# Two weight sums of a Strassen product in buffers of their own

## The chip, the cores and the metric

The kernel runs on one core of a Trainium2 chip. The metric is the device time of one execution in microseconds (us). Before the change it was 2573.67 us, the median of 3 runs (2573.44 to 2575.31).

The engines of the core work on their own, each through a list of instructions in a fixed order, and wait for each other by semaphores: PE multiplies matrices into PSUM, DVE and POOL work elementwise, ACT casts and applies functions, SP issues the transfers from and to HBM.

## What is computed

One layer of a streaming encoder on 512 frames of 2048 channels, all in float32: a combined input projection, stick-breaking attention, a spatial gating unit, two output projections and a squared-ReLU MLP. The change lies in the MLP, which is the last of it:

```python
D_MODEL = 2048
SEQ = 512
D_FF = 4 * D_MODEL

        x = x + merged @ w_out[l]

        h2 = rms_norm(x, g_ff[l])
        x = x + jnp.square(jax.nn.relu(h2 @ w_ff1[l])) @ w_ff2[l]
```

## The kernel before

**Two parts for each operand.** PE multiplies in a shorter float type. So each operand is split into a rounded part, hi, and the rest, lo: ACT casts the block to hi and DVE subtracts hi from the block (`split_to`, lines 103 and 104; for weights of the other products `weight`, lines 90 and 92). A product is three matmuls, hi by hi, hi by lo and lo by hi (`mm3`, lines 68 to 70). Which of lines 69 and 70 reads the weights' lo depends on the side on which the weights stand: in `strassen` it is line 69 (weights on the right), in the first MLP product line 70.

**The MLP's loop** (lines 631 to 649) runs over 16 chunks of 512 hidden channels. In each chunk, twice (g = 0 and 1, here the even and the odd product): `hidden` computes 256 channels of the next chunk (four weight loads, 96 matmuls; a relu on DVE, line 603, and a square on ACT, line 604), and then `strassen` multiplies the current chunk by a block of w_ff2 of 512 rows and 1024 columns and adds it into x. The last chunk has no `hidden`.

**The Strassen product** (lines 140 to 188) is Winograd's form: seven products of quarters instead of eight. The four quarters w11, w12, w21, w22 of the weights are loaded with SP in this order (line 156). The seven products stand in a fixed order, y11, y21, m7, m6, y22, m4, m5, with 12 matmuls each. y11, m4 and y21 take w11, w22 and w12 as they are loaded. The other four take sums of quarters that POOL makes by `plus` (line 165):

- m7 takes w11 + w21, written in the place of w11
- m6 takes that sum + w22, in a buffer of its own, sc
- y22 takes sc + w12, written in the place of w12
- m5 takes w21 + w22, written in the place of w21

Each is recorded right ahead of the product that takes it. A sum in the place of w11 has to wait until w11 has been split for y11.

Products y11, m6 and m5 accumulate in one pair of PSUM banks, m7 and m4 in another; y21 and y22 use a third, one after the other. After each product, `evac_y` adds the banks into x (line 643, on DVE), for m5 twice; the next product on the same banks adds to them once DVE has read them. The pieces w_hi and w_lo go round in 6 buffers, so three blocks are in flight.

**The other factors** (`factors`, lines 610 to 625) are made once a chunk: POOL makes four sums of the activations for each of two pairs (lines 615 to 618), and ACT and DVE split 7 factors of each pair (ys, 128x256). These fall into the odd product of the chunk before, since the activations are ready only there.

**What sets the order.** The program is written in the order above, and a scheduler then fixes the order of each engine's list with a timing model of its own. Buffers come from pools. A pool hands its buffers out again in the order in which they come free, and who takes one waits for the last reader of what was in it. The pool `slots` has 72 buffers of 128x512, of which x takes 16, the normed input of the MLP 32, and the rest goes round among activations, sums and factors. The pool `spare` (10 such buffers, for the first transposed inputs and the last merged blocks) is given up ahead of the MLP, and the pool `whole` (line 590: 5 buffers of 128x1024, for the four quarters and sc) takes its place.

## Time and profile before

| | |
|---|---|
| median of 3 runs | 2573.67 us |
| the profiled execution, its own time | 2574.17 us |
| its span, first to last instruction | 2572.5 us |
| granted clock of PE | 1.0 |
| instructions | 28610 |
| share of 16 DMA engines' time on loads | 32.7% |

The page has six parts: busy time by engine; the span in 40 slices; DMA queues; the chain of work that ended last; the costliest groups of instructions; and DMA issues. A group's row names the line, engine, operation, output<-inputs with their shape, and how many; behind the first bar its busy time in us and the mean of one in ns; behind the second the engine's idle time just before these instructions and what ended it. A row of the timeline gives start and length in us, engine, line, operation, tiles, how many such instructions follow each other, and in brackets the idle time before it. A matmul's length in the rows is longer than the step from one to the next, since matmuls are pipelined.

### The profile page before, as it was taken

The page shows a single profiled execution, that of the slowest core. Times are in us where ns is not written, and L with a number is a line of the kernel's source. Part 1 is how long each engine was busy: PE and PEld are TensorE (multiplying, and loading weights), DVE is VectorE, ACT ScalarE, POOL GpSimd, SP SyncE. Part 2 cuts the span into 40 slices and gives each one's busy share as a digit, 9 for nine tenths or more (in the row PEclk, how much of TensorE's full clock was granted, in tenths as well). Part 3 has the DMA queues.
Part 4 walks back from the last instruction along what each step waited for, and adds up shares of the span by engine and source line. Part 5 has one row for each costly group of instructions (what it writes and reads, how often), then busy time and mean ns, then how long its engine had stood idle before and what let it go on. Part 6 is the DMA issues. An engine that isn't in the chain of part 4 may idle for free.

```text
span 2572.5 us, 28610 instructions
## 1 busy us (share of the span) xinstructions
PE 2532.1 (98%) x11306; PEld 2082.1 (81%) x11306; DVE 1438.7 (56%) x1806; ACT 852.9 (33%) x1172; POOL 589.0 (23%) x379
## 2 busy tenths in 40 slices
PE   8999999999999999999999999999999999999998
PEld 7888888888888888888878777887778777877786
DVE  4555563333335333333475767667666767576759
ACT  5333342222223222223333333333332334233333
POOL 0211110000211000100223242414342333324244
PEclk9999999999999999999999999999999999999999
DMA  5332323333332333434233323233323333332323
GB/s 172 90 91 74 90 64 99 93 97 98 115 115 78 99 101 93 129 107 133 88 110 95 115 87 111 89 115 97 101 90 107 102 95 99 98 115 82 114 68 121
DMA packets 169574, 259.83 MB, mean 101 GB/s; under 512 B 8368, under 2 KB 77024, under 8 KB 169440
## 3 DMA queue, kind: packets, MB, share of 16 engines
q1 hardware_dynamic: 169440, 258.01, 32.7%
q8 instruction: 89, 1.46, 0.2%
q14 instruction: 45, 0.37, 0.0%
HBM read 253.78 MB, written 4.19 MB: 100 GB/s over the span
## 4 chain that ended last, share of the span: by engine, by line
PE 87%; DVE 10%; issue 1%; ACT 1%; DMA 0%; POOL 0%; SPq 0%; DVEq 0%; ACTq 0%; POOLq 0%
PE f L69 9%; PE f L68 9%; PE f L70 9%; PE q L69 6%; PE q L70 6%; PE q L68 6%; DVE w_lo L104 4%; DVE ys L104 3%; DVE x L643 3%; PE xo L70 2%; PE xo L69 2%; PE xo L68 2%; PE gb L68 2%; PE gb L70 2%; PE gb L69 2%; PE ga L68 2%
## 5 line engine op out<-in xcount | busy, mean ns | idle before, releaser
L92 DVE TENSOR_TENSOR w_lo<-w_raw,w_hi 128x1024 fp32r<-128x1024 f32 x336 | 414.2, 1233 | 686.5 <-ACT w_hi L90 677.7
L90 ACT CAST w_hi<-w_raw 128x1024 fp32r<-128x1024 f32 x336 | 353.7, 1053 | 988.8 <-PE q L69 190.0
L104 DVE TENSOR_TENSOR w_lo<-w_raw,w_hi 128x1024 fp32r<-128x1024 f32 x192 | 281.9, 1469 | 255.8 <-ACT w_hi L103 255.8
L68 PE MATMUL f<-h2T_hi,w_hi 128*128 128x512 f32 x1024 | 398.6, 389 | 0.0
L69 PE MATMUL f<-h2T_lo,w_hi 128*128 128x512 f32 x1024 | 398.5, 389 | 0.0
L70 PE MATMUL f<-h2T_hi,w_lo 128*128 128x512 f32 x1024 | 397.9, 391 | 0.0
L69 PE MATMUL q<-w_lo,ys 128*128 128x512 f32 x896 | 352.8, 394 | 26.4 <-DVE w_lo L104 26.3
L165 POOL TENSOR_TENSOR w_raw<-w_raw 128x1024 f32<-128x1024 f32 x64 | 183.1, 2862 | 820.0 <-DVE w_lo L104 820.0
L70 PE MATMUL q<-w_hi,ys 128*128 128x512 f32 x896 | 349.0, 389 | 0.0
L643 DVE TENSOR_TENSOR x<-x,q 128x512 f32<-128x512 f32 x512 | 331.0, 676 | 2.3 <-PE q L70 0.6
L103 ACT CAST w_hi<-w_raw 128x1024 fp32r<-128x1024 f32 x192 | 201.8, 1053 | 391.2 <-PE f L69 290.3
L68 PE MATMUL q<-w_hi,ys 128*128 128x512 f32 x896 | 324.0, 391 | 1.5 <-DVE x L643 1.2
L69 PEld LDWEIGHTS q<-w_lo,ys 128*128 128x128 f32 x896 | 168.1, 188 | 74.1 <-DVE w_lo L104 40.0
L70 PEld LDWEIGHTS f<-h2T_hi,w_lo 128*128 128x128 f32 x1024 | 192.2, 188 | 44.2 <-DVE w_lo L92 4.6
L69 PEld LDWEIGHTS f<-h2T_lo,w_hi 128*128 128x128 f32 x1024 | 192.2, 188 | 40.1
L68 PEld LDWEIGHTS f<-h2T_hi,w_hi 128*128 128x128 f32 x1024 | 192.3, 188 | 39.4
L68 PEld LDWEIGHTS q<-w_hi,ys 128*128 128x128 f32 x896 | 168.1, 188 | 40.3 <-issue 3.5
L70 PEld LDWEIGHTS q<-w_hi,ys 128*128 128x128 f32 x896 | 168.3, 188 | 33.8
L68 PE MATMUL gb<-hT_hi,w_hi 128*128 128x512 f32 x256 | 100.3, 392 | 0.2 <-DVE gb L413 0.2
L68 PE MATMUL xo<-w_hi,mT_hi 128*128 128x512 f32 x256 | 100.5, 393 | 0.0
L68 PE MATMUL ga<-hT_hi,w_hi 128*128 128x512 f32 x256 | 100.4, 392 | 0.0
L69 PE MATMUL ga<-hT_lo,w_hi 128*128 128x512 f32 x256 | 100.0, 391 | 0.0
(199 smaller groups left out, 3919.4 us busy)
## 6 DMA issues: line engine op xcount, KB each, us to landing
w_raw<-in_w_ff_dram SPq DMA_DIRECT2D x256, 512.0 KB, 3.7
w_raw<-in_w_in_dram SPq DMA_DIRECT2D x144, 512.0 KB, 3.7
w_raw<-in_w_out_dram SPq DMA_DIRECT2D x32, 512.0 KB, 3.7
w_raw<-in_w_oa_dram SPq DMA_DIRECT2D x16, 512.0 KB, 3.7
w_raw<-in_w_ob_dram SPq DMA_DIRECT2D x16, 512.0 KB, 3.6
x<-in_x_dram SPq DMA_DIRECT2D x16, 256.0 KB, 5.3
out_dram<-x SPq DMA_DIRECT2D x16, 256.0 KB, 2.2
xq<-in_x_dram SPq DMA_DIRECT2D x12, 256.0 KB, 6.4
```

What stands on the lines that cost most here:

```text
L68: nc.tensor.matmul(o, lhsT=lh[0], rhs=rh[0], start=start, stop=False, **kw)
L69: nc.tensor.matmul(o, lhsT=lh[0], rhs=rh[1], start=False, stop=False, **kw)
L70: nc.tensor.matmul(o, lhsT=lh[1], rhs=rh[0], start=False, stop=stop, **kw)
L90: nc.scalar.copy(out=hi, in_=raw)
L92: nc.vector.tensor_tensor(out=lo, in0=raw, in1=f32(hi), op=ALU.subtract)
L103: nc.scalar.copy(out=hi, in_=src)
L104: nc.vector.tensor_tensor(out=lo, in0=src, in1=f32(hi), op=ALU.subtract)
L165: nc.gpsimd.tensor_tensor(out=o, in0=a, in1=b, op=ALU.add)
L643: nc.vector.tensor_tensor(out=a, in0=a, in1=o, op=op)
```

## The change

Two of the four sums get buffers of their own. w11 + w21 goes to a new buffer, sa, so w11 stays whole, and the sum for m6 is made from sa. All sums but that for y22 are recorded ahead of the first product, and so depend on loads alone and on a free buffer; the sum for y22, which still goes in the place of w12, is recorded behind w12's split for y21. The order of the products, the operands of each product and the number of sums stay as they were. The pool `whole` has 6 buffers instead of 5. For that, `spare` has 12 and `slots` 70; the transposed inputs in `spare` are 6 pairs instead of 5.

```diff
-SLOTS = 72
-SPARE = 10
+SLOTS = 70
+SPARE = 12
...
-        sc = whole("w_sum")
+        sa, sc = whole("w_sum"), whole("w_sum")
...
-        made = {"m7": lambda: plus(w11, w11, w21), "m6": lambda: plus(sc, w11, w22),
-                "y22": lambda: plus(w12, sc, w12), "m5": lambda: plus(w21, w21, w22)}
-        take = {"y11": w11, "y21": w12, "m7": w11, "m6": sc, "y22": w12, "m4": w22, "m5": w21}
+        plus(sa, w11, w21)
+        plus(sc, sa, w22)
+        plus(w21, w21, w22)
+        take = {"y11": w11, "y21": w12, "m7": sa, "m6": sc, "y22": w12, "m4": w22, "m5": w21}
...
-            if name in made:
-                made[name]()
             hi, lo = piece("w_hi"), piece("w_lo")
             split_to(hi, lo, take[name])
+            if name == "y21":
+                plus(w12, sc, w12)
...
-    state["whole"] = ctx.enter_context(tc.tile_pool(name="whole", bufs=5))
+    state["whole"] = ctx.enter_context(tc.tile_pool(name="whole", bufs=6))
```

Lines behind the constants and ahead of the loop of products keep their numbers; from there on, a line has a number higher by one (643 becomes 644).

How this moves instructions is shown at three places. All are in one chunk, around its odd product, the one that starts at 1912.55 us in the profile of before; numbers behind a name tell buffers apart.

POOL, from the last sum of the factors to the next product's weight sums; in brackets the semaphores waited for (DMAHW those of loads). Before:

```order
L617 TENSOR_TENSOR m_13789<-relu_13609,m_13788 128x256 [waits Pool_49]
L165 TENSOR_TENSOR w_raw_13943<-w_raw_13943,w_raw_13947 128x1024 [waits DMAHW7_49,DMAHW1_49,DVE_49]
L165 TENSOR_TENSOR w_sum_13951<-w_raw_13943,w_raw_13949 128x1024 [waits DMAHW2_49,Pool_49]
L165 TENSOR_TENSOR w_raw_13947<-w_raw_13947,w_raw_13949 128x1024
L165 TENSOR_TENSOR w_raw_13945<-w_sum_13951,w_raw_13945 128x1024 [waits DMAHW0_49,DVE_49,Pool_49]
```

Now:

```order
L618 TENSOR_TENSOR m_13805<-relu_13624,m_13804 128x256 [waits Pool_49]
L165 TENSOR_TENSOR w_sum_13967<-w_raw_13959,w_raw_13963 128x1024 [waits DMAHW7_49,DMAHW1_49,DVE_49]
L165 TENSOR_TENSOR w_raw_13963<-w_raw_13963,w_raw_13965 128x1024 [waits DMAHW2_49,Pool_49]
L165 TENSOR_TENSOR w_sum_13968<-w_sum_13967,w_raw_13965 128x1024 [waits DVE_49]
L165 TENSOR_TENSOR w_raw_13961<-w_sum_13968,w_raw_13961 128x1024 [waits DMAHW0_49,DVE_49,Pool_49]
```

The sum for m5 has moved ahead of that for m6. The first sum's wait for DVE was one for the split of w11 of its own product; now it is one for the split of w22 (for m4) of the product before, whose buffer it takes. The third sum waits likewise for the split for m5 of the product before. The last, for y22, waits for w12's split of its own product, as before.

DVE in the odd product, from the split for m4 to that for m5 (w_lo from w_raw; ys are the next factors, x2 the additions into x). Before:

```order
L104 TENSOR_TENSOR w_lo_13723<-w_raw_13618,w_hi_13722 128x1024
L104 TENSOR_TENSOR ys_13803<-m_13788,ys_13803 128x256
L104 TENSOR_TENSOR ys_13806<-relu_13609,ys_13806 128x256
L104 TENSOR_TENSOR ys_13809<-m_13789,ys_13809 128x256
L643 TENSOR_TENSOR x2_8284<-x2_8284,q_13626 128x512
L104 TENSOR_TENSOR w_lo_13742<-w_raw_13616,w_hi_13741 128x1024
```

Now:

```order
L104 TENSOR_TENSOR w_lo_13740<-w_raw_13633,w_hi_13739 128x1024
L104 TENSOR_TENSOR ys_13810<-relu_13621,ys_13810 128x256
L104 TENSOR_TENSOR ys_13813<-relu_13624,ys_13813 128x256
L104 TENSOR_TENSOR ys_13816<-m_13804,ys_13816 128x256
L644 TENSOR_TENSOR x2_8282<-x2_8282,q_13644 128x512
L104 TENSOR_TENSOR ys_13819<-m_13804,ys_13819 128x256
L644 TENSOR_TENSOR x2_8284<-x2_8284,q_13645 128x512
L104 TENSOR_TENSOR w_lo_13758<-w_raw_13631,w_hi_13757 128x1024
```

Three factors and the addition of m6's first tile, which stood ahead of m4's split, now stand behind it. From the split for m7 to that for m4 DVE's list was: the split for m7, 2 additions, the split for m6, a factor, an addition, 4 factors, an addition, 2 factors, the split for y22, an addition, a factor, an addition, 2 factors, an addition, the split for m4. It is now: the split for m7, 2 additions, 3 factors, an addition, the split for m6, 3 factors, an addition, the split for y22, a factor, 2 additions, the split for m4.

DVE from the split for m5 to the first split of the hidden product that follows (line 92). Before:

```order
L104 TENSOR_TENSOR w_lo_13742<-w_raw_13616,w_hi_13741 128x1024
L104 TENSOR_TENSOR ys_13812<-m_13789,ys_13812 128x256
L643 TENSOR_TENSOR x2_7986<-x2_7986,q_13706 128x512
L643 TENSOR_TENSOR x2_7988<-x2_7988,q_13707 128x512
L92 TENSOR_TENSOR w_lo_13821<-w_raw_13817,w_hi_13819 128x1024
```

Now:

```order
L104 TENSOR_TENSOR w_lo_13758<-w_raw_13631,w_hi_13757 128x1024
L644 TENSOR_TENSOR x2_7986<-x2_7986,q_13723 128x512
L104 TENSOR_TENSOR ys_13822<-relu_13624,ys_13822 128x256
L104 TENSOR_TENSOR ys_13825<-m_13805,ys_13825 128x256
L104 TENSOR_TENSOR ys_13828<-m_13805,ys_13828 128x256
L644 TENSOR_TENSOR x2_7988<-x2_7988,q_13724 128x512
L92 TENSOR_TENSOR w_lo_13837<-w_raw_13833,w_hi_13835 128x1024
```

Three factors are left for this stretch where one was. On PE, y22's and m4's matmuls keep their pattern (both banks by hi, then lo). At the end of the odd product PE's list is now: m5's first matmul on one bank, two matmuls of the hidden product, m5's first on the other bank, then m5's other ten. SP's list of loads is the same; w11 now takes the buffer of the w11 before, w12 that of sa, w21 that of sc, and w22 that of w12.

## The prediction

> **What bounds the kernel now.** I read the page's first and fourth part, then the groups, then the timeline of one stretch of the second MLP product.

> ```profile
> PE 2532.1 (98%) x11306; PEld 2082.1 (81%) x11306; DVE 1438.7 (56%) x1806; ACT 852.9 (33%) x1172; POOL 589.0 (23%) x379
> ...
> PE 87%; DVE 10%; issue 1%; ACT 1%; DMA 0%; POOL 0%; SPq 0%; DVEq 0%; ACTq 0%; POOLq 0%
> ...
> L69 PE MATMUL q<-w_lo,ys 128*128 128x512 f32 x896 | 352.8, 394 | 26.4 <-DVE w_lo L104 26.3
> ...
> L165 POOL TENSOR_TENSOR w_raw<-w_raw 128x1024 f32<-128x1024 f32 x64 | 183.1, 2862 | 820.0 <-DVE w_lo L104 820.0
> ```

> PE is busy 98% of the span, so little can be won: the span less PE's busy time is 40.4 us. Of that, 26.3 us are waits for the splits of the blocks of the second product (w_lo, line 104). POOL's 820.0 us of waiting for a split, which the change addresses by name, is idle time of an engine that is busy 23%, and costs nothing by itself.

> The end follows from how long a chunk of the last loop takes. The timeline of PE shows where three chunks in a row start their second product of the odd kind (g = 1):

> ```profile
> 1828.52 0.39 PE L68 MATMUL q<-w_hi,ys 128*128 128x512 f32 x1
> ...
> 1912.55 0.39 PE L68 MATMUL q<-w_hi,ys 128*128 128x512 f32 x1
> ...
> 1994.77 0.39 PE L69 MATMUL f<-h2T_lo,w_hi 128*128 128x512 f32 x1
> ...
> 1996.58 0.39 PE L68 MATMUL q<-w_hi,ys 128*128 128x512 f32 x1
> 1996.81 0.39 PE L69 MATMUL q<-w_lo,ys 128*128 128x512 f32 x1
> ```

> A chunk lasts 84.03 us, both times. From 1994.77 to 1996.81 there are nine steps from matmul to matmul, so one takes 0.2267 us. A chunk has 360 (two hidden products of 96, two Strassen products of 84), 81.6 us. So 2.4 us are lost in each chunk, and they are lost in the product that starts at 1912.55, which I call S:

> ```profile
> 1923.43 0.61 PE L68 MATMUL q<-w_hi,ys 128*128 128x512 f32 x2
> 1924.99 0.50 PE L69 MATMUL q<-w_lo,ys 128*128 128x512 f32 x1 [0.94 <-DVE w_lo L104]
> ...
> 1927.41 0.94 PE L68 MATMUL q<-w_hi,ys 128*128 128x512 f32 x3
> 1928.92 0.50 PE L69 MATMUL q<-w_lo,ys 128*128 128x512 f32 x1 [0.58 <-DVE w_lo L104]
> ```

> At y22 the third matmul could start at 1923.43 + 0.45 and starts 1.11 us later; at m4 the fourth could start at 1927.41 + 0.68 and starts 0.83 later. That is 1.94 of the 2.4. Both wait for DVE, and DVE waits there for nothing: it works through a queue of splits (w_lo), splits of the next factors (ys) and additions into x, and its neighbour POOL slows it.

> **How DVE and POOL get in each other's way.** First POOL's rows of this stretch, then DVE's:

> ```profile
> 1906.51 2.40 POOL L165 TENSOR_TENSOR w_sum<-w_raw 128x1024 f32<-128x1024 f32 x1
> 1908.86 3.39 POOL L165 TENSOR_TENSOR w_raw<-w_raw 128x1024 f32<-128x1024 f32 x1
> 1912.21 2.40 POOL L165 TENSOR_TENSOR w_raw<-w_sum,w_raw 128x1024 f32<-128x1024 f32 x1
> ...
> 1918.75 0.81 POOL L617 TENSOR_TENSOR m<-relu,m 128x256 f32<-128x256 f32 x1
> ```

> ```profile
> 1908.17 1.82 DVE L104 TENSOR_TENSOR w_lo<-w_raw,w_hi 128x1024 fp32r<-128x1024 f32 x1 [4.21 <-ACT w_hi L103]
> ...
> 1913.66 2.03 DVE L104 TENSOR_TENSOR w_lo<-w_raw,w_hi 128x1024 fp32r<-128x1024 f32 x1 [0.22 <-ACT w_hi L103]
> 1915.62 1.27 DVE L643 TENSOR_TENSOR x<-x,q 128x512 f32<-128x512 f32 x2
> 1916.81 1.26 DVE L104 TENSOR_TENSOR w_lo<-w_sum,w_hi 128x1024 fp32r<-128x1024 f32 x1
> ...
> 1918.88 0.67 DVE L643 TENSOR_TENSOR x<-x,q 128x512 f32<-128x512 f32 x1
> ...
> 1919.81 1.84 DVE L104 TENSOR_TENSOR ys<-m,ys 128x256 fp32r<-128x256 f32 x2
> 1921.57 0.96 DVE L104 TENSOR_TENSOR ys<-relu,ys 128x256 fp32r<-128x256 f32 x1
> ...
> 1923.05 0.75 DVE L104 TENSOR_TENSOR ys<-m,ys 128x256 fp32r<-128x256 f32 x2
> 1923.72 1.21 DVE L104 TENSOR_TENSOR w_lo<-w_raw,w_hi 128x1024 fp32r<-128x1024 f32 x1
> 1924.86 0.68 DVE L643 TENSOR_TENSOR x<-x,q 128x512 f32<-128x512 f32 x1
> ```

> Alone, a split takes 1.21 us (1923.72). The one at 1908.17 takes 1.82: it gets through only when the sum that POOL began at 1906.51 ends at 1908.91. The next sum begins at 1908.86 and takes 3.39 instead of 2.40: it moves only when that split ends, at 1909.99. So the two take turns, a whole instruction each. After 1909.99 the sum needs until 1912.25: it bars DVE for **2.2 us**. A small factor sum of POOL bars it for 0.55: two splits of factors take 1921.57 - 1919.81 = 1.76 us beside POOL's factor sums and 1923.72 - 1923.05 = 0.67 without them, 0.88 against 0.335 each. An addition into x reads PSUM and isn't barred: 0.67 at 1918.88, inside the POOL instruction of 1918.75. In a row of its own, DVE steps on by 1.14 for a split (1923.72 to 1924.86) and by 0.60 for an addition (1915.62 to 1916.81, two).

> [...]

> **The change, part by part.** It removes and adds no instruction on PE, DVE, ACT or POOL and no load; it moves them.

> *The sums.* Before, the four sums for a product wait for the split of its first block, and the first three run during the hidden product, where DVE has slack (idle 4.21 us before the split of 1908.17). Now three of them need only loads and a free buffer. The buffers go round in the order of release: the first sum takes that of w22, free when m4 of the product before is split; the second needs the load of w22; the third takes that of w21, free when m5 is split. The load of w21 is issued behind the split for m6 and lands long before that:

> ```profile
> w_raw<-in_w_ff_dram SPq DMA_DIRECT2D x256, 512.0 KB, 3.7
> ```

> So three sums leave the quiet hidden product and run **in the middle of the product before it**, from m4's split on, one after another, on DVE's busiest stretch.

> *Before m4.* By the new order I add up DVE's queue in the odd product. The split for m7 starts, as now, behind ACT's cast, at S + 1.11; it ends at 2.25, since no sum bars it. The second addition waits for the product y11, whose last matmul starts at S + 2.5 and ends 0.39 later: 2.9 to 3.5. From there to the end of m4's split stand 7 splits of factors (2.35), 4 additions (2.4), 3 block splits (3.4), and POOL's factor sums, of which I let two bar for their whole 0.55 and one for 0.1 (1.2; in the nearest rows, from 1919.81 to 1922.45, three of three do): S + 12.85. Products start every 12 x 0.2267 = 2.72 us. y22's split is through at 9.65 and needed at 10.88 + 0.45; m4's is through at 12.85 and needed at 14.05. **Both old stalls go.** The bounds of the barring are 0 and 7 x 0.55: m4's split comes 1.2 earlier or 2.65 later; all that follows moves with it.

> *After m4.* One split of a factor passes (13.2). Then the first sum bars until 15.4, a factor passes (15.75), the second sum bars until 17.95, a factor passes (18.3). The addition of m6's first tile ends at 18.9, a factor at 19.2, the second addition at 19.8, the split for m5 at 20.95. PE is due for m5 at S + 16.3. Its first matmul adds into the bank that the first addition reads: it waits until 18.9, 2.6 us. Two matmuls of the hidden product stand next, then m5's on the other bank (0.25 lost), then the first that needs the split: 0.95 lost. In all 3.8, and m5 ends at 23.25.

> *The hidden product.* Its third matmul needs a split on DVE. From 20.95: an addition (21.55), the third sum bars until 23.25, three factors (24.25), an addition (24.85), the split (26.0). PE comes there at 23.25: 2.8 lost. The next split is needed 5 us later, and there DVE is in time.

> So a chunk loses 6.6 us in place of 2.4: **+4.2**. In the even product there are no factors to split; one sum delays m5's split by about 1 us, and it has 2 us to spare, since three pieces are in flight: I take nothing.

> *The other two edits.* The main pool has 70 slots, not 72, so new factors wait for older ones to be used up; ACT casts them ahead of the blocks. The cast for m6 then ends by S + 3.75 for a use at 8.6: hidden, by nearly 5 us. At the program's start the order of transposes and squares moves a little. PE idles there for the first loads, which stay:

> ```profile
> L276 PE MATMUL xT<-ident,xk 128*128 128x128 f32 x16 | 4.1, 424 | 4.3 <-DMA xk<-in_x_dram 4.3
> L226 PE MATMUL gp<-ident,gm 16*128 16x16 f32 x1 | 0.3, 256 | 2.7 <-DMA gm<-in_g_mix_dram 2.7
> ```

> I take nothing for it, and at most 2 us either way.

> *The end.* The last odd product but one starts at 1912.55 + 7 x 84.03 = 2500.8. From the first, at 1324.3, there are 14 chunks: 14 x 4.2 = 58.8. Behind 2500.8 there is no hidden product, and ACT waits for sums:

> ```profile
> L69 PE MATMUL q<-w_lo,ys 128*128 128x512 f32 x84 | 33.6, 400 | 5.1 <-DVE w_lo L104 5.0
> ...
> L68 PE MATMUL q<-w_hi,ys 128*128 128x512 f32 x84 | 30.2, 392 | 1.5 <-DVE x L643 1.2 <-ACT w_hi L103 0.2
> ...
> L103 ACT CAST w_hi<-w_raw 128x1024 fp32r<-128x1024 f32 x16 | 16.5, 1050 | 28.0 <-POOL w_raw L165 13.9 <-PE q L69 11.4 <-DVE x L643 1.5
> ```

> PE loses 6.6 us there (these groups are from 2500 us on). Sums that are ready earlier take some of it away: I take -3, between -6.6 and +5.

> Sum: 58.8 - 3 = +56. The profiled run took 2574.17 us (span 2572.5), the median of the three runs 2573.67: **2629**.

> **The rivals.** [...] 0.07. (2) *The change doesn't do what it says:* w21's load comes so late that the sums still run in the hidden product. It would have to land 6 us after its issue behind m6's split (S + 6.4), not 3.7. Then 2545 to 2575. 0.04. (3) *Partly:* the barring falls on other instructions and costs about what is won, 2570 to 2600; 0.05. (4) *Slower still:* the two missing slots hold back a cast on ACT, and with it m4's split; each us costs 14: 2645 to 2660. The cast would have to lose its 5 us first. 0.06.

> **How the numbers follow.** The forecast has 0.78. The hold is between 2.0 and 2.4 (8 us either way), the queue before m4 between -1.2 and +2.65 per chunk (-17, +37), the end between -4 and +8; not all at one end. So 2600 to 2652, which leaves out rivals 1 to 3 and a little of the forecast, 0.18 in all. About 0.2% can be told from no change here. Slower: 0.78 + 0.06 + 0.02 of rival 3 = 0.86; within 0.2%: 0.03 of rival 3 and 0.02 of rival 2, 0.05; faster: 0.07 + 0.02 = 0.09.

> **What would show it.** A chunk of 88.2 us instead of 84.03; no wait of PE at y22 and m4, but one at m5 for an addition (line 644) and one of the hidden product's matmul on line 70 for line 92; POOL's sums of 2.4 us or more beginning 13 us after the odd product's start, with splits of factors of over 2 us beside them; and POOL's wait for w_lo shorter than 820. Splits of 0.4 us beside such sums would make the prediction wrong, and so would sums that still start in the hidden product.

## The result, and the profile after

The changed kernel takes **2640.37 us** (median of four runs, 2634.77 to 2642.11); the kernel before took 2573.93 beside it (2573.44 to 2575.31). The ratio is 1.0253, with a 95% interval of 1.0236 to 1.0271: slower. The profiled run is the shortest of the four, 2634.77, with a span of 2632.7; 60.2 us more than the span before.

First the page of the changed kernel: the engines' busy time, the chain that ended last, and three groups of PE's matmuls (busy us, mean ns, then PE's idle time ahead of them and who ended it).

```profile
PE 2555.9 (97%) x11306; PEld 2097.1 (80%) x11306; DVE 1506.7 (57%) x1806; ACT 856.8 (33%) x1172; POOL 600.5 (23%) x379
...
PE 82%; DVE 13%; issue 3%; ACT 1%; DMA 0%; POOL 0%; SPq 0%; DVEq 0%; ACTq 0%; POOLq 0%
...
L70 PE MATMUL f<-h2T_hi,w_lo 128*128 128x512 f32 x1024 | 401.0, 394 | 23.2 <-DVE w_lo L92 23.2
...
L69 PE MATMUL q<-w_lo,ys 128*128 128x512 f32 x896 | 357.7, 399 | 11.2 <-DVE w_lo L104 11.1
...
L68 PE MATMUL q<-w_hi,ys 128*128 128x512 f32 x896 | 329.9, 398 | 30.0 <-DVE x L644 29.5
```

The 26.3 us of waiting for splits of blocks (line 104) went down to 11.1. Two new waits came: 29.5 for the addition into x (line 644) and 23.2 for the hidden product's split (line 92). Besides, PE's busy time rose by 23.8 us for the same 11306 matmuls. Most of it comes from "half-clock" matmuls: 83 that step on by 0.427 us instead of 0.2267, 16.6 us in all (the granted clock is 0.50 there, as for the 9 matmuls from 1700.66 to 1704.08); the last section is about them. POOL's waits, from the view that groups waits (us in all, how often, the longest):

```profile
POOL w_raw L165 <- issue: 578.1, 31, 23.2
POOL w_sum L165 <- DVE w_lo L104: 219.4, 31, 11.2
```

The 820.0 us that POOL's sums waited for splits are 219.4 now. POOL isn't idle for less time, though: 578.1 us more stand ahead of the sum for y22, which still waits for w12's split and which the view puts under "issue". What changed is the place: three of the four sums now run in another stretch, and the kernel lost by it. One odd product shows how. PE first, from the product's start S = 1944.55 to the start of the next chunk's odd product:

```profile
1944.55 0.39 PE L68 MATMUL q<-w_hi,ys 128*128 128x512 f32 x1
...
1963.17 0.48 PE L68 MATMUL q<-w_hi,ys 128*128 128x512 f32 x1 [2.14 <-DVE x L644]
...
1965.15 0.80 PE L69 MATMUL q<-w_lo,ys 128*128 128x512 f32 x1 [0.21 <-DVE w_lo L104]
...
1970.30 0.50 PE L70 MATMUL f<-h2T_hi,w_lo 128*128 128x512 f32 x1 [1.80 <-DVE w_lo L92]
...
2032.58 0.39 PE L68 MATMUL q<-w_hi,ys 128*128 128x512 f32 x1
```

A chunk of 88.03 us. No wait at y22 and m4 is left; PE waits at m5, for an addition and then for the split, and in the hidden product's third matmul. POOL in the same stretch, and DVE:

```profile
1946.09 1.60 POOL L618 TENSOR_TENSOR m<-relu,m 128x256 f32<-128x256 f32 x1
...
1952.59 2.11 POOL L619 TENSOR_TENSOR m<-relu 128x256 f32<-128x256 f32 x1
...
1955.48 1.61 POOL L618 TENSOR_TENSOR m<-relu,m 128x256 f32<-128x256 f32 x1
1957.05 2.58 POOL L165 TENSOR_TENSOR w_sum<-w_raw 128x1024 f32<-128x1024 f32 x1
1959.71 2.43 POOL L165 TENSOR_TENSOR w_raw<-w_raw 128x1024 f32<-128x1024 f32 x1
1965.17 2.38 POOL L165 TENSOR_TENSOR w_sum<-w_sum,w_raw 128x1024 f32<-128x1024 f32 x1 [3.03 <-DVE w_lo L104]
```

```profile
1952.56 1.21 DVE L104 TENSOR_TENSOR w_lo<-w_raw,w_hi 128x1024 fp32r<-128x1024 f32 x1
1953.69 0.41 DVE L104 TENSOR_TENSOR ys<-m,ys 128x256 fp32r<-128x256 f32 x1
...
1955.22 1.26 DVE L104 TENSOR_TENSOR w_lo<-w_raw,w_hi 128x1024 fp32r<-128x1024 f32 x1
1956.41 3.50 DVE L104 TENSOR_TENSOR ys<-relu,ys 128x256 fp32r<-128x256 f32 x2
1959.84 2.59 DVE L104 TENSOR_TENSOR ys<-m,ys 128x256 fp32r<-128x256 f32 x1
1962.35 0.68 DVE L644 TENSOR_TENSOR x<-x,q 128x512 f32<-128x512 f32 x1
...
1963.88 1.21 DVE L104 TENSOR_TENSOR w_lo<-w_raw,w_hi 128x1024 fp32r<-128x1024 f32 x1
...
1965.62 2.22 DVE L104 TENSOR_TENSOR ys<-relu,ys 128x256 fp32r<-128x256 f32 x1
...
1969.03 1.21 DVE L92 TENSOR_TENSOR w_lo<-w_raw,w_hi 128x1024 fp32r<-128x1024 f32 x1
```

The first sum begins 12.5 us after S, and each of the three sums has one split of a factor beside it that gets through only as it ends: 3.50 for a pair, 2.59 and 2.22 for one. DVE's queue behind them is late.

### The profile page after: what moved, and what is told of

It reads as the page before. It is cut to its first block, busy times and chain, and to the rows that moved or that the text cites. A ratio compares the mean times of both kernels' runs of the same rounds, so it can differ in the third digit from the quotient of the medians.

```text
span 2632.7 us, 28646 instructions
## 1 busy us (share of the span) xinstructions
PE 2555.9 (97%) x11306; PEld 2097.1 (80%) x11306; DVE 1506.7 (57%) x1806; ACT 856.8 (33%) x1172; POOL 600.5 (23%) x379
## 4 chain that ended last, share of the span: by engine, by line
PE 82%; DVE 13%; issue 3%; ACT 1%; DMA 0%; POOL 0%; SPq 0%; DVEq 0%; ACTq 0%; POOLq 0%
PE f L70 9%; PE f L69 9%; PE f L68 9%; DVE ys L104 5%; PE q L68 5%; PE q L69 5%; PE q L70 5%; DVE x L644 4%; DVE w_lo L104 3%; PE xo L70 2%; PE xo L69 2%; PE xo L68 2%; PE gb L68 2%; PE gb L70 2%; PE gb L69 2%
## 5 line engine op out<-in xcount | busy, mean ns | idle before, releaser
L92 DVE TENSOR_TENSOR w_lo<-w_raw,w_hi 128x1024 fp32r<-128x1024 f32 x336 | 446.3, 1328 | 653.9 <-ACT w_hi L90 642.2
L90 ACT CAST w_hi<-w_raw 128x1024 fp32r<-128x1024 f32 x336 | 353.6, 1052 | 1056.2 <-PE q L69 225.4
L70 PE MATMUL f<-h2T_hi,w_lo 128*128 128x512 f32 x1024 | 401.0, 394 | 23.2 <-DVE w_lo L92 23.2
L68 PE MATMUL f<-h2T_hi,w_hi 128*128 128x512 f32 x1024 | 402.1, 393 | 0.0
L69 PE MATMUL f<-h2T_lo,w_hi 128*128 128x512 f32 x1024 | 401.9, 393 | 0.0
L69 PE MATMUL q<-w_lo,ys 128*128 128x512 f32 x896 | 357.7, 399 | 11.2 <-DVE w_lo L104 11.1
L104 DVE TENSOR_TENSOR w_lo<-w_raw,w_hi 128x1024 fp32r<-128x1024 f32 x160 | 216.3, 1352 | 252.4 <-ACT w_hi L103 252.4
L68 PE MATMUL q<-w_hi,ys 128*128 128x512 f32 x896 | 329.9, 398 | 30.0 <-DVE x L644 29.5
L70 PE MATMUL q<-w_hi,ys 128*128 128x512 f32 x896 | 354.3, 395 | 0.0
L103 ACT CAST w_hi<-w_raw 128x1024 fp32r<-128x1024 f32 x160 | 168.8, 1055 | 371.0 <-PE f L69 254.6
L70 PEld LDWEIGHTS f<-h2T_hi,w_lo 128*128 128x128 f32 x1024 | 194.0, 189 | 70.4 <-DVE w_lo L92 30.2
L68 PEld LDWEIGHTS q<-w_hi,ys 128*128 128x128 f32 x896 | 170.7, 190 | 74.9 <-issue 33.5
L69 PEld LDWEIGHTS f<-h2T_lo,w_hi 128*128 128x128 f32 x1024 | 194.2, 190 | 40.9
L68 PEld LDWEIGHTS f<-h2T_hi,w_hi 128*128 128x128 f32 x1024 | 194.2, 190 | 39.5
L69 PEld LDWEIGHTS q<-w_lo,ys 128*128 128x128 f32 x896 | 171.8, 192 | 56.1 <-DVE w_lo L104 20.7
L165 POOL TENSOR_TENSOR w_raw<-w_sum,w_raw 128x1024 f32<-128x1024 f32 x32 | 76.8, 2401 | 591.2 <-issue 578.1
L70 PEld LDWEIGHTS q<-w_hi,ys 128*128 128x128 f32 x896 | 171.9, 192 | 35.3
L165 POOL TENSOR_TENSOR w_sum<-w_raw 128x1024 f32<-128x1024 f32 x32 | 79.7, 2491 | 189.1 <-DVE w_lo L104 176.8
L165 POOL TENSOR_TENSOR w_sum<-w_sum,w_raw 128x1024 f32<-128x1024 f32 x32 | 91.5, 2858 | 44.0 <-DVE w_lo L104 42.7
L68 PE MATMUL gb<-hT_hi,w_hi 128*128 128x512 f32 x256 | 100.3, 392 | 0.2 <-DVE gb L414 0.2
L104 DVE TENSOR_TENSOR ys<-relu,ys 128x256 fp32r<-128x256 f32 x96 | 100.5, 1072 | 0.0
## 6 DMA issues: line engine op xcount, KB each, us to landing
w_raw<-in_w_ff_dram SPq DMA_DIRECT2D x256, 512.0 KB, 3.7
w_raw<-in_w_in_dram SPq DMA_DIRECT2D x144, 512.0 KB, 3.7
w_raw<-in_w_out_dram SPq DMA_DIRECT2D x32, 512.0 KB, 3.7
w_raw<-in_w_oa_dram SPq DMA_DIRECT2D x16, 512.0 KB, 3.7
w_raw<-in_w_ob_dram SPq DMA_DIRECT2D x16, 512.0 KB, 3.7
```

What stands on the lines that cost most here:

```text
L68: nc.tensor.matmul(o, lhsT=lh[0], rhs=rh[0], start=start, stop=False, **kw)
L69: nc.tensor.matmul(o, lhsT=lh[0], rhs=rh[1], start=False, stop=False, **kw)
L70: nc.tensor.matmul(o, lhsT=lh[1], rhs=rh[0], start=False, stop=stop, **kw)
L90: nc.scalar.copy(out=hi, in_=raw)
L92: nc.vector.tensor_tensor(out=lo, in0=raw, in1=f32(hi), op=ALU.subtract)
L103: nc.scalar.copy(out=hi, in_=src)
```

## The experiments

Nine kernels ran. "Chunk" is the time from one odd product's start to the next, as most of the 14 show it; the ratio is to the kernel before on the same chip.

| kernel | us, median | ratio, 95% interval | chunk |
|---|---|---|---|
| before | 2573.93 | | 84.03 |
| changed | 2640.37 | 1.0253, 1.0236 to 1.0271 | 88.03 (10 of 14), 89.0 to 90.1 (4) |
| before, with 70 slots and 12 spare | 2566.11 | 0.9971, 0.9960 to 0.9982 | 83.5 |
| before, with 70 slots | 2566.60 | 0.9970, 0.9959 to 0.9982 | 83.5 |
| changed, early sums left out | 2535.15 | 0.9850, 0.9836 to 0.9865 | 81.8 |
| early sums for odd products only | 2541.41 | 0.9875, 0.9858 to 0.9891 | 81.8 |
| the same, sizes of before | 2549.46 | 0.9907, 0.9892 to 0.9922 | 82.4 |
| early sums for even products only | 2645.48 | 1.0279, 1.0263 to 1.0294 | 89.1 |
| changed, sums in four pieces | 2589.10 | 1.0058, 1.0043 to 1.0073 | 84.4 (5), 86.0 (9) |
| changed, early sums on DVE | 2557.89 | 0.9937, 0.9921 to 0.9954 | 82.9 |
| changed, five block buffers, 72 slots | 2568.82 | 0.9978, 0.9969 to 0.9988 | 83.6 |

**Without the early sums.** This kernel leaves out three of the four block sums of each product, so it computes something else and serves for its time alone.

```diff
-        sa, sc = whole("w_sum"), whole("w_sum")
...
-        plus(sa, w11, w21)
-        plus(sc, sa, w22)
-        plus(w21, w21, w22)
-        take = {"y11": w11, "y21": w12, "m7": sa, "m6": sc, "y22": w12, "m4": w22, "m5": w21}
+        take = {"y11": w11, "y21": w12, "m7": w11, "m6": w22, "y22": w12, "m4": w22, "m5": w21}
...
-                plus(w12, sc, w12)
+                plus(w12, w22, w12)
```

> The changed kernel without its three early sums: m7, m6 and m5 are multiplied by blocks as loaded (w11, w22, w21), so three of the seven block sums are left out of the computation. Theory: without the three holds of 2.2 us DVE is in time again at m5 (its queue is then through at about S + 16.6, PE due at S + 16.3) and late by some 0.5 us in the hidden product; the chunk is 81.6 + 0.8 = 82.4 us instead of 88.0, the sum 2574 - 14 x 1.6 = 2551, between 2538 and 2560; no matmul step of 0.427 us, granted clock 1.0. Rival (it is DVE's new order and not the sums that makes m5 and the hidden product late): both waits stay, 2620 or more.

Measured: 2535.15 us, a chunk of 81.8, no half-clock matmul in the profiled loop (granted clock 0.999 to 1.0 in its runs). Both waits went with the sums, so DVE's order is not their cause. The time is 3 us under the expected range and 16 under the 2551 in it: the chunk is 0.6 us shorter than I expected, since nearly nothing is lost in the hidden product (14 x 0.6 = 8.4), and from the start of the last odd product but one to the end of the span it takes 64.3 us where the kernel before takes 71.7.

**One half each.** The early sums for the even products (g = 0) run in the odd product ahead, those for the odd ones in the even product ahead. Against the changed kernel:

```diff
-        sa, sc = whole("w_sum"), whole("w_sum")
+        own = g == 1
+        sa = whole("w_sum") if own else w11
+        sc = whole("w_sum")
...
-        plus(sa, w11, w21)
-        plus(sc, sa, w22)
-        plus(w21, w21, w22)
+        made = {"m7": lambda: plus(sa, w11, w21), "m6": lambda: plus(sc, sa, w22),
+                "y22": lambda: plus(w12, sc, w12), "m5": lambda: plus(w21, w21, w22)}
+        if own:
+            for name in ("m7", "m6", "m5"):
+                made.pop(name)()
...
+            if name in made and not (own and name == "y22"):
+                made[name]()
...
-            if name == "y21":
-                plus(w12, sc, w12)
+            if own and name == "y21":
+                made["y22"]()
```

> Only the odd products (g = 1) have buffers of their own and early sums; their sums run in the even product before, where no factors are split. The even products make theirs in the place of a split block, as before the change, so in the hidden product behind the odd one. Theory: the stalls of y22 and m4 go (1.94 us of each chunk) and those of m5 and the hidden product do not come: a chunk of 82.1, 2574 - 14 x 1.94 = 2547, between 2538 and 2555, granted clock 1.0. Rival (early sums cost wherever they run, by the buffers' going round or the new order): slower than 2574.

The other half has `own = g == 0`.

> The opposite half: only the even products (g = 0) have early sums, which run in the middle of the odd product; the odd products make theirs as before the change, in the hidden product ahead. Theory: both losses meet in the odd product: the sum that bars the split for m7 is back (y22 and m4 late by 1.9 us in all) and the three sums behind m4 stay (6.4 us): a chunk of 81.6 + 1.9 + 6.4 = 89.9, 2574 + 14 x 5.9 = 2656 and up to 10 us more by half-clock matmuls, between 2645 and 2675. Rival (the loss comes from the early sums of both kinds alike): halfway, about 2607.

Measured: 2541.41 and 2645.48. The even products' sums make the whole loss, and the odd products' sums alone make the kernel **faster than both**, by 1.25% against the one before. The rivals are out: early sums don't cost wherever they run, and the loss isn't shared. The odd-only kernel is also the best control for the changed one, since DVE's rows of the odd product stand in the same order in both. PE's rows at the start of two of its chunks, and DVE's rows that answer to those above (S = 1896.72):

```profile
1896.72 0.39 PE L68 MATMUL q<-w_hi,ys 128*128 128x512 f32 x1
...
1978.52 0.39 PE L68 MATMUL q<-w_hi,ys 128*128 128x512 f32 x1
```

```profile
1907.40 1.26 DVE L104 TENSOR_TENSOR w_lo<-w_raw,w_hi 128x1024 fp32r<-128x1024 f32 x1
1908.59 1.29 DVE L104 TENSOR_TENSOR ys<-relu,ys 128x256 fp32r<-128x256 f32 x2
1909.81 0.41 DVE L104 TENSOR_TENSOR ys<-m,ys 128x256 fp32r<-128x256 f32 x1
...
1913.41 0.41 DVE L104 TENSOR_TENSOR ys<-relu,ys 128x256 fp32r<-128x256 f32 x1
...
1915.01 1.21 DVE L92 TENSOR_TENSOR w_lo<-w_raw,w_hi 128x1024 fp32r<-128x1024 f32 x1
```

m4's split starts at S + 10.68 here and at S + 10.67 in the changed kernel. Then the same three rows take 1.29, 0.41 and 0.41 in place of 3.50, 2.59 and 2.22: 2.21 + 2.18 + 1.81 = 6.20 us. The hidden product's split starts at S + 18.29 here and at S + 24.48 there, 6.19 later, and the chunks are 81.80 and 88.03, 6.23 apart. So what the chunk loses is what POOL's three sums hold DVE, to a few hundredths.

The even-only kernel came out at the low end of its range (a chunk of 89.1 against 89.9), but not as I expected it to. The old stalls didn't come back: in the chunk that starts at 1947.89 PE doesn't wait at y22, and at m4 it loses under 0.3 us. It waits at m5 and in the hidden product, there also for a cast on ACT (line 90, 16.2 us in 12 waits), which ran behind the held splits. The holds account for the chunk all the same:

```profile
1962.58 4.75 DVE L104 TENSOR_TENSOR ys<-relu,ys 128x256 fp32r<-128x256 f32 x2
...
1970.59 2.00 DVE L104 TENSOR_TENSOR ys<-m,ys 128x256 fp32r<-128x256 f32 x1
```

A pair takes 4.75 instead of 0.75 and a single split 2.00 instead of 0.41: 5.6 us of holds. The kernel before with 70 slots, which is the next experiment, has a chunk of 83.5, and 83.5 + 5.6 = 89.1.

**The sizes alone.** The kernel before with `SLOTS = 70` and `SPARE = 12`, and once with 70 slots alone.

> The kernel before with 70 slots and 12 spare ones, nothing else. Theory (the POOL sums bar DVE): the slots cost nothing, since the first hidden product starts at 1283.47 us after the change and at 1283.41 before it; 2574 us, within 4, and a chunk of 84.0. Rival (part of the 60 us is the two missing slots, which hold back casts of factors on ACT): 2590 or more, a chunk of 85 or more.

> The kernel before with 70 slots, and with its 10 spare ones. Tells which size gave the 7.6 us: theory (the slots: splits of factors start later, and splits of blocks get ahead of them in the odd product, chunk 83.5 instead of 84.0): 2566. Rival (the 12 spare slots at the program's start): 2574.

Measured: 2566.11 and 2566.60. Here **my theory of the first fell, and so did its rival**: two slots fewer make the kernel faster by 7.5 us; the spare slots do nothing that can be told. The loop shows it: with 70 slots DVE splits y22's block here (PE's start of the odd product first, then DVE's row):

```profile
1908.63 0.39 PE L68 MATMUL q<-w_hi,ys 128*128 128x512 f32 x1
```

```profile
1917.51 1.21 DVE L104 TENSOR_TENSOR w_lo<-w_raw,w_hi 128x1024 fp32r<-128x1024 f32 x1
```

That is S + 8.88; before it was 1923.72 - 1912.55 = S + 11.17. With fewer slots five splits of factors stand ahead of it where seven stood, which is 0.67 of the 2.29 us. The rest is three holds by POOL's factor sums, which are gone there: the pair that took 1.84 us before (at 1919.81) takes 0.75.

```profile
1915.90 0.75 DVE L104 TENSOR_TENSOR ys<-m,ys 128x256 fp32r<-128x256 f32 x2
```

The two splits come behind y22's, and the hidden product then waits some 0.9 us a chunk, where it waited for nearly nothing before.

To see whether this is part of the odd-only kernel's gain, that kernel ran with five block buffers, 72 slots and 10 spare ones:

> Early sums for the odd products alone, as in the run that took 2541 us, but with the 72 slots, 10 spare ones and five block buffers of the kernel before. Theory (what counts is that no sum bars DVE in the odd product): the chunk is at its floor of 81.8 us with the old sizes too, 2541, between 2536 and 2547. Rival (the 7.6 us that two slots fewer gave by themselves are part of that gain): 2549.

Measured: 2549.46. The rival's number: at m5 0.37 us is lost with 72 slots, and the chunk is 82.4. So the slots are worth 8 us there too.

**The same sums, narrower, and on DVE.**

```diff
-            nc.gpsimd.tensor_tensor(out=o, in0=a, in1=b, op=ALU.add)
+            for k in range(KH):
+                for c in range(0, W, 256):
+                    o_, a_, b_ = (t[:, k, c:c + 256] for t in (o, a, b))
+                    nc.gpsimd.tensor_tensor(out=o_, in0=a_, in1=b_, op=ALU.add)
```

> The changed kernel with each of the four sums made in four pieces of 256 columns instead of one of 1024. Theory (the two engines take turns, a whole instruction each, so a hold is as long as one POOL instruction): a piece holds DVE for some 0.55 us, and between the first sum and the hidden product's first split stand nine instructions of DVE that can be held; 9 x 0.5 = 4.5 us at most, less where a piece runs beside an addition into x, so 3.5 to 4.5 instead of the 6.2 by which the chunk is longer now than with the odd products' sums alone (88.0 against 81.8). A chunk of 85.3 to 86.3, 2541 + 14 x 4 = 2597, between 2585 and 2608; splits of factors of about 0.9 us, and none of over 2. Rival (what counts is POOL's work in this stretch, however it is cut): 6.2 us stay, 2635 or more.

```diff
-            nc.gpsimd.tensor_tensor(out=o, in0=a, in1=b, op=ALU.add)
+            nc.vector.tensor_tensor(out=o, in0=a, in1=b, op=ALU.add)
...
-                plus(w12, sc, w12)
+                nc.gpsimd.tensor_tensor(out=w12, in0=sc, in1=w12, op=ALU.add)
```

> The changed kernel with its three early sums made by DVE itself, in its own queue; only y22's sum stays on POOL. Theory (it is POOL's hold of 2.2 us, not the sum being early, that costs): a sum costs DVE the 1.14 us of a split. One of them stands ahead of m5's split, two behind the hidden product's first split, which has 5 us until the next is needed. So a chunk of 81.8 + 1.1 = 82.9, 2541 + 14 x 1.1 = 2557, between 2545 and 2575: faster than before the change, although DVE does more. Rival (any early sum in the odd product costs, as DVE is full there): three sums of 1.14 to 2.2 us in the chunk, 2590 or more.

Measured: 2589.10 and 2557.89, both inside their ranges; the first for a reason that was half wrong. Its chunks come in two lengths, 84.4 and 86.0. DVE in one of 84.4 (S = 1581.16):

```profile
1593.45 1.84 DVE L104 TENSOR_TENSOR ys<-relu,ys 128x256 fp32r<-128x256 f32 x2
1595.21 0.96 DVE L104 TENSOR_TENSOR ys<-m,ys 128x256 fp32r<-128x256 f32 x1
...
1599.69 1.83 DVE L104 TENSOR_TENSOR ys<-m,ys 128x256 fp32r<-128x256 f32 x2
...
1602.05 1.21 DVE L92 TENSOR_TENSOR w_lo<-w_raw,w_hi 128x1024 fp32r<-128x1024 f32 x1
```

The pair that took 1.29 in the odd-only kernel takes 1.84, the single split 0.96 instead of 0.41: one hold of 0.55 each, beside pieces of 256 columns. The later pair takes 1.83 instead of 0.75, two holds. The hidden product's split starts at S + 20.89, 2.60 later than in the odd-only kernel, and 84.4 - 81.8 is 2.6: 0.55 + 0.55 + 1.08, and 0.42 by which the split for m7 takes longer (1.84 against 1.42). So the hold goes with the width of one POOL instruction (0.55 us at 256 columns, 1.81 to 2.21 at 1024), but only four of the nine instructions that I counted were held by pieces; the others took their usual 0.34 or 1.2 us. That alone would have given 2541 + 14 x 2.6 = 2578. The rest comes from the nine chunks of 86.0, which the clock makes (0.51 granted behind the wait, worth 1.6 us; last section).

With the sums on DVE one stands ahead of m5's split (S = 1903.79 in this chunk):

```profile
1918.70 1.21 DVE L165 TENSOR_TENSOR w_sum<-w_raw 128x1024 f32<-128x1024 f32 x1
1919.83 1.21 DVE L104 TENSOR_TENSOR w_lo<-w_raw,w_hi 128x1024 fp32r<-128x1024 f32 x1
...
1923.17 1.21 DVE L92 TENSOR_TENSOR w_lo<-w_raw,w_hi 128x1024 fp32r<-128x1024 f32 x1
```

It costs the 1.13 us by which m5's split steps back, and the chunk is 82.9. The three early sums of all 32 products on the engine that everybody waits for are 82 us cheaper in all than on the one that is idle three quarters of the time.

**The same sums a little later.** With five block buffers in place of six (and 72 slots) the early sums wait one split longer for a free buffer.

> The changed kernel with five block buffers instead of six, and so with 72 slots and 10 spare ones: all six early sums as in the change, but the buffers come free one split later. Theory (the place counts): the sums for the even product then start behind the split for m5 and not behind that for m4, two of them at the beginning of the hidden product and the third about a product of four buffers later, where DVE has time; m5 is not late, and the hidden product is late by at most one to two us: a chunk between 82 and 84, 2555, between 2541 and 2575. Rival (early sums for the even product cost the 6.2 us wherever they stand): 2625 or more.

Measured: 2568.82, inside the range. POOL and PE in the odd product that starts at 1909.13:

```profile
1926.94 2.39 POOL L165 TENSOR_TENSOR w_sum<-w_raw 128x1024 f32<-128x1024 f32 x1 [8.56 <-DVE w_lo L104]
1929.41 3.26 POOL L165 TENSOR_TENSOR w_raw<-w_raw 128x1024 f32<-128x1024 f32 x1
1943.40 2.39 POOL L165 TENSOR_TENSOR w_sum<-w_sum,w_raw 128x1024 f32<-128x1024 f32 x1 [10.73 <-DVE w_lo L104]
```

```profile
1930.47 0.50 PE L70 MATMUL f<-h2T_hi,w_lo 128*128 128x512 f32 x1 [0.99 <-DVE w_lo L92]
```

The first two sums start at S + 17.8 instead of S + 12.5, and the third 14 us behind the second. PE's wait for line 644 is gone, the wait for line 92 is 0.99. Five microseconds of place, with the clock that came with the longer waits (0.984 to 0.990 in the changed kernel's runs, 0.998 to 1.0 in these; last section), are worth 72 us of the kernel's time, although this kernel lacks what the two slots fewer give. With 72 slots the order of DVE's splits of factors is another too, so the place is not the only difference.

## Why the prediction was right in its sign and its mechanism, and 11 us short

*The old stalls.* Both went, as forecast. y22's split was through at 1953.77, S + 9.2 (forecast 9.65), m4's at S + 11.9 (12.85). The term that was too large is the barring by POOL's factor sums ahead of m4, which I had put at 1.2 us: the rows show some 0.1. The first pair's factor sums are through at 1946.09 + 1.60, S + 3.1, ahead of all splits of factors. Those of the second pair do run beside DVE's splits, but there POOL waits: the sum that begins at 1952.59 takes 2.11 instead of the 0.75 that the first pair's took at 1944.57, and ends at 1954.70, behind the block split of 1952.56 and the factor split of 1953.69. So the two engines don't always take turns one by one, as I had read from the rows of before; here two splits in a row passed a waiting sum.

*The new stalls.* The three sums start at S + 12.5 (forecast 13.2), two in a row and the third behind m5's split, and hold 2.21, 2.18 and 1.81 us: the size, and here the turn-taking too, were as read from the trace of before. m5's first matmul came at S + 18.62 (forecast 18.9), its split was through at S + 20.5 (20.95), the hidden product's at S + 25.7 (26.0). The chunk is **88.03 against a forecast of 88.2**. That it is so near is in part luck: m4's split was through 0.9 us earlier than forecast, and then the pair of 3.50 lost another 0.55 to the factor sum of 1955.48, which I hadn't counted there (the odd-only kernel has the same hold, 1.29 instead of 0.75). The even product lost nothing, as forecast: from its start to that of the odd product it is 40.80 us in both kernels. The forecast's range allowed for holds of 2.0 to 2.4 us; none in this chunk came to 2.4. The held time was 2.21, 2.18 and 1.81 us beside sums of 2.58, 2.43 and 2.38 us, and 0.55 where they were cut in four.

*The end.* Forecast -3; from the start of the last odd product but one to the span's end it is 2632.7 - 2562.7 = 70.0 against 71.7 before, so -1.7.

*The other two edits.* That the slots cost nothing was **wrong**: 70 slots make the kernel before 7.5 us faster. This didn't spoil the sum, because DVE's queue was added up from the new order, which the scheduler had made with 70 slots. The rival that said the slots would hold something back had the wrong sign: they do hold back the factors, and that helps. By the runs, in this order, the chunk's +4.0 is -0.5 (slots), -1.7 (the odd products' sums) and +6.2 (the even products').

*The term that is missing: the clock.* 14 chunks of 88.03 and the end give 14 x 4.0 - 1.7 = 54 and a time near 2628, next to the forecast of 2629. The forecast put nothing for PE's clock. The profiled run is 6 us longer, as four of its chunks are 89.0 to 90.1. Chunk by chunk, worked out from the starts of the odd products, with the number of matmuls that stepped on by 0.427 us instead of 0.2267:

```
us     88.04 88.00 89.85 89.37 88.02 89.02 88.04 88.03 88.03 87.99 88.02 87.99 88.01 90.08
0.427      0     5    16     5     7     7     0     3     4     6     7     3     3    17
```

Where such steps fall ahead of the hidden product's wait, they cost nothing, as DVE is later than PE anyway (chunks of 88.0 have up to 7 of them); behind it they lengthen the chunk. The other three runs are 4.6 to 7.3 us longer than the profiled one, at a granted clock of 0.984 to 0.986 instead of 0.990. That their difference has the same cause is argued from these clocks, not seen, as only one run has a trace.

The rivals: that sums beside DVE's full queue cost it nothing, for which 0.07 stood, and that the loss and the gain about cancel (3) are out by the holds of 2.21, 2.18 and 1.81; that loads come late (2), by sums that start at S + 12.5; that a cast is held back (4), by the slots' run and by PE's waits for line 103 in the changed kernel, 0.4 us in all. Rival 4's 2645 to 2660 lies near the measured 2640, but its mechanism didn't add the 11 us: by the trace 6 of them are the clock's, and for the rest that is argued.

## What to carry to other kernels

A wait of an idle engine is worth nothing by itself (POOL's for splits went from 820.0 us to 219.4 here, and the kernel lost 66), and what it does when the wait is taken away can cost: look first at what will run beside it (here sums on POOL that held splits on DVE by 1.81 to 2.21 us). Move such work to the stretch where the other engine has time (here: early sums for the odd products alone, 1.25% faster than before, 0.9% with the old sizes), cut it into narrower instructions (which here took back 51 of the 66 us lost, and stayed slower than before), or give it to the busy engine itself if that does it in half the time (1.21 us against 2.40). And try each size on its own that a change alters by the way: two slots fewer were worth 0.3%, and not because of what the change was made for.

## What the runs showed that I had not expected

**The same wait of 2.02 us, with half the clock behind it or with the full one.** In the kernel with narrow sums each chunk has the same wait of PE, 2.02 us longer than a step, in the hidden product's third matmul. In nine of 14 chunks seven matmuls of 0.427 us follow, in five none. The windows ahead of and behind that wait in one chunk of each kind (columns: stretch, its length, PE's busy time and matmuls, granted clock, DMA's share, GB/s), then PE's rows:

```profile
1514.00:1517.40 3.40, 1.54 (x8) 1.00 0.00 0
1517.40:1520.80 3.40, 3.40 (x8) 0.51 0.52 156
1600.00:1603.40 3.40, 1.54 (x8) 1.00 0.00 0
1603.40:1606.80 3.40, 3.40 (x15) 1.00 0.54 157
```

```profile
1517.34 0.71 PE L70 MATMUL f<-h2T_hi,w_lo 128*128 128x512 f32 x1 [1.86 <-DVE w_lo L92]
1517.84 0.63 PE L68 MATMUL f<-h2T_hi,w_hi 128*128 128x512 f32 x1
1518.27 0.63 PE L69 MATMUL f<-h2T_lo,w_hi 128*128 128x512 f32 x1
```

```profile
1603.31 0.50 PE L70 MATMUL f<-h2T_hi,w_lo 128*128 128x512 f32 x1 [1.86 <-DVE w_lo L92]
1603.65 0.39 PE L68 MATMUL f<-h2T_hi,w_hi 128*128 128x512 f32 x1
1603.88 0.40 PE L69 MATMUL f<-h2T_lo,w_hi 128*128 128x512 f32 x1
```
